# Stick-breaking attention on one core: the order of VectorE, ScalarE and GpSimd written out, v turned inside the score banks, weight units prepared in three steps, 51 tiles for activations

## Chip, core and metric

The kernel runs on one NeuronCore of a Trainium2 chip. The metric is the device time of one execution in microseconds (us). All arithmetic is float32: where TensorE takes part, a value is split into a high part (rounded to the matmul's fp32r format) and a low part (what the rounding left), and a product is three matmuls: low weight times high activation, high times low, high times high.

## The reference, cut to what matters

A decoder trunk of two layers over 512 tokens of width 1024: a Mamba-2 layer, then a stick-breaking attention layer with 16 heads of 64. Each layer ends with a convolutional GLU feed-forward (2816 wide) and a gated per-layer embedding. K and V come from the normed output of layer 0. The part that the change touches:

```python
def stick_breaking_attention(q, k, v):
    scale = SB_HEAD_DIM ** -0.5
    for blk in range(seq // SB_BLOCK):
        ...
        z = jnp.einsum("bthd,bshd->bhts", q[:, q0:q1], k[:, :q1]).astype(jnp.float32) * scale
        causal = (q0 + jnp.arange(SB_BLOCK))[:, None] > jnp.arange(q1)[None, :]
        log_beta = jax.nn.log_sigmoid(z)
        log_keep = jnp.where(causal, jax.nn.log_sigmoid(-z), 0.0)
        log_rest = lax.cumsum(log_keep, axis=3, reverse=True) - log_keep
        w = jnp.where(causal, jnp.exp(log_beta + log_rest), 0.0)
        outs.append(jnp.einsum("bhts,bshd->bthd", w.astype(v.dtype), v[:, :q1]))
```

## The kernel before

Activations lie transposed, features on the 128 partitions and the 512 tokens along the free axis, so that one activation tile is 128x512 float32. All weights stream once from HBM as 240 units of eight 128x128 blocks (512 KB each) in the order in which TensorE uses them (`PLAN`). `Weights.make` loads a unit into `raw` (three buffers, queue of SyncE), multiplies in the gain of a norm where the unit belongs to q, k or v (L95, GpSimd, one instruction for a whole unit), copies it to `whi` (L106, ScalarE) and writes the rest to `wlo` (L107, VectorE). `product` adds up one 128x512 output tile in a bank of PSUM, three matmuls for each 128 rows (L217 to L219), so a unit is 24 matmuls.

In attention a pair is two heads, and there are eight pairs. PSUM has eight banks: two rotating `acc` banks for projections, four `aux` banks and the two banks of `two`. For one pair the kernel makes the scores in five tiles `z` (`scores`: tile 0 takes columns 0 to 255 of both banks of `two`, tiles 1 to 4 an `aux` bank each); ScalarE takes Abs and Exp of each tile (L805, L806), then Ln (L809); VectorE forms softplus (L812) and rounds it (`sh`, L816), and GpSimd writes the rest (`sl`, L817); TensorE adds the cumulative sums into the same banks (`att_b`, L844); ScalarE takes Exp (L847) and rounds (`wh`, L849), VectorE writes the rest (`wl`, L850). The output matmuls of a pair (`att_c`, one call for each head, L868) are issued in the stretch of the next pair, and are evacuated by a ScalarE copy (L873) and a VectorE add (L874).

TensorE's order is written out by hand, for the whole kernel. In the stretch of a middle pair p it is: scores(p), att_c of pair p-1 for head 0, the projection k(p+1), att_c for head 1, the projection q(p+1) with the four transposes of v (L748) after its fourth step, att_b(p), the projection v(p+1). Each of `pav`, k, `pav`, q, `pv` (the transposed v) and v takes the next `acc` bank, in turns of two. k and q are evacuated by one VectorE instruction (L736) that multiplies with the norm's `n_kv.r`, then split by L198 (ScalarE) and L199 (VectorE). The order on VectorE, ScalarE and GpSimd is found by the framework's list scheduler, from the program's order, priorities (`high_priority`) and estimated times. Ahead of the pairs, layer 0's gate phase (`layer_tail`, L687 to L706: one projection a tile, then L694, L695, L698, L701, and the norm's running sum L236 on GpSimd) hands over to q(0), k(0) and k(1); between them come the norm's `sums` (L243) and `spread` (L278), whose result scales q and k.

Of the kernel before, what the change touches and what calls it, by code (L numbers as in the profile page):

```python
# [15 lines left out]
P = 128  # L16
T = 512
NCH = 4
# [49 lines left out]
class Weights:  # L68
# [3 lines left out]
    def __init__(self, tc, pool, src, ahead=2):  # L72
        self.tc, nc = tc, tc.nc
        self.nc, self.pool, self.src, self.ahead = nc, pool, src, ahead
        self.units, self.made, self.pos, self.gains = {}, 0, 0, {}

    def make(self, u, between=None):
        nc = self.nc
# [21 lines left out]
        name = PLAN[8 * u][0]  # L100
        hi = self.pool.tile([P, 8, P], F32R, tag="whi", name="whi", bufs=3)
        lo = self.pool.tile([P, 8, P], F32R, tag="wlo", name="wlo", bufs=3)
        for c, part in enumerate(parts):
            e = nc.gpsimd if u == 0 and c else nc.vector
            with self.tc.high_priority(offset=120) if name == "in" and u > 2 else nullcontext():
                nc.scalar.copy(out=hi[:, part], in_=raw[:, part])  # L106
                e.tensor_tensor(out=lo[:, part], in0=raw[:, part], in1=hi[:, part].bitcast(F32), op=ALU.subtract)  # L107
        self.units[u] = (hi, lo)

    def next(self, what):  # L110
        assert PLAN[self.pos] == what, (PLAN[self.pos], what)
        u, i = divmod(self.pos, 8)
        while self.made < min(NUNIT, u + 1 + self.ahead):
            self.make(self.made)
            self.made += 1
# [6 lines left out]
def tile_yoco(ctx: ExitStack, tc: tile.TileContext, xT, pT, prm, cst, csb, wdt, wts, out, dbg=None):  # L122
# [24 lines left out]
    def H(dt=F32, shape=(P, T), name="h"):  # L147
        return sb.tile(list(shape), dt, tag="H", name=name, bufs=44)
# [31 lines left out]
    wt.made = 1  # L180
# [546 lines left out]
    qs, ks, vs = {}, {}, {}  # L727
# [6 lines left out]
    def qk_split(dst, p, acc, scale):  # L734
        t = S("t", 2)
        V.scalar_tensor_tensor(out=t, in0=acc, scalar=scale, in1=n_kv.r, op0=ALU.mult, op1=ALU.mult)  # L736
        dst[p] = split(t)

    def v_evac(p, acc):
        t = S("t", 2, name="v")  # L740
        V.tensor_tensor(out=t, in0=acc, in1=n_kv.r, op=ALU.mult)
        vs[p] = t

    def v_split(p):
        t = vs[p]
        pv = acc_bank("pv")
        for c in range(NCH):
            PE.transpose(out=pv[:, c * P:(c + 1) * P], in_=t[:, c * P:(c + 1) * P], identity=ident)  # L748
        pv4 = pv.rearrange("p (c i d) -> p c i d", c=NCH, i=2)
        vs[p] = []  # L750
        for i in range(2):
            vv = H(F32R, shape=(P, NCH, 2, 64), name="vv")
            A.copy(out=vv[:, :, 0], in_=pv4[:, :, i])
            V.tensor_tensor(out=vv[:, :, 1], in0=pv4[:, :, i], in1=vv[:, :, 0].bitcast(F32), op=ALU.subtract)
# [6 lines left out]
    def scores(p):  # L761

        two = two_banks("z")
# [35 lines left out]
    def att_a(p):  # L799

        es, sp = {}, {}
        zs = scores(p)
        for n in (2, 0, 1, 3, 4):
            e = es[n] = S("d", 6, name="e") if n < 3 else S("c", 3, name="e")
            A.activation(out=like(n, e), in_=zs[n], func=AF.Abs)  # L805
            last = A.activation(out=e, in_=e, func=AF.Exp, scale=-1.0)  # L806
        with tc.issue_after(last.ins):
            for n in (2, 0, 1, 3, 4):
                ln = A.activation(out=es[n], in_=es[n], func=AF.Ln, bias=1.0)  # L809
        for n in (2, 0, 1, 3, 4):  # L810
            e = es[n]
            V.scalar_tensor_tensor(  # L812
                out=like(n, e), in0=zs[n], scalar=0.0, in1=like(n, e), op0=ALU.max, op1=ALU.add
            )
            hi, lo = H(F32R, name="sh"), H(F32R, name="sl")
            V.tensor_copy(out=hi, in_=e)  # L816
            G.tensor_tensor(out=lo, in0=e, in1=hi.bitcast(F32), op=ALU.subtract)  # L817
            sp[n] = (hi, lo)
        return zs, sp, ln

    def att_b(p, zs, sp, ln):
# [10 lines left out]
        for n in (1, 0, 2, 3, 4):  # L832
# [12 lines left out]
            w = S("c", 3, name="w")  # L845
            with tc.issue_after(ln.ins):
                A.activation(out=like(n, w), in_=z, func=AF.Exp)  # L847
            hi, lo = H(F32R, name="wh"), H(F32R, name="wl")
            A.copy(out=hi, in_=w)  # L849
            V.tensor_tensor(out=lo, in0=w, in1=hi.bitcast(F32), op=ALU.subtract)  # L850
            ws[n] = (hi, lo)
# [6 lines left out]
    def att_c(p, i, ws, bank=acc_bank):  # L858

        if i == 0:  # L860
            ots[p] = S("e", 3)
        ot = ots[p]
# [4 lines left out]
        for n, (o_, l_, r_) in enumerate(mm):  # L867
            PE.matmul(  # L868
                o_, lhsT=l_.rearrange("p a d -> p (a d)"), rhs=r_, start=n == 0, stop=n == len(mm) - 1,
            )  # L870
        tp = S("th", 1, name="tp")
        with tc.high_priority(offset=300):
            A.copy(out=tp[0:64], in_=po[64:128])  # L873
            V.tensor_tensor(out=ot[LO[i]], in0=po[0:64], in1=tp[0:64], op=ALU.add)  # L874
        if i:
            if dbg:
                dbg("o", p, ot)
            o_t.append(split(ot, lo=S("ot", 8, F32R)))

    def qk(name, dst, p, scale, hooks=None):  # L880
        acc = proj(name, p, hooks)
        with tc.high_priority(offset=200):
            qk_split(dst, p, acc, scale)

    def v_proj(p):
        acc = proj("v", p)
        with tc.high_priority(offset=200):
            v_evac(p, acc)
# [6 lines left out]
    qk("k", ks, 1, 1.0, hooks={3: n_kv.spread})  # L895
    with tc.high_priority(offset=400):
        qk_split(qs, 0, qa, 0.125)
        qk_split(ks, 0, ka, 1.0)
    ws = None
    for p in range(8):  # L900
        zz = att_a(p)
# [120 lines left out]
```

## Time and profile before

| what | us |
|---|---|
| three timed executions | 1584.12, 1590.03, 8543.81 (median 1590.03) |
| the profiled execution's own time | 1585.07 |
| its span, first to last instruction | 1583.1 |
| TensorE busy in it | 1508.4 (95%) |
| VectorE, ScalarE, GpSimd busy | 1020.1, 754.4, 344.3 |
| the eight pairs of attention, 842.45 to 1108.00 | 265.55 |

The profile is of one execution. A matmul's end is modelled, so two matmuls in a row overlap in it, and what one costs is read from the distance of their starts. The profile's clock column is TensorE's granted clock as a share of 2.4 GHz: 0.50 is 1.2 GHz.

### The profile page before, as it was taken

To read this page: it belongs to the slowest core of one execution; us is meant where nothing else is said; L and a number is where in the kernel's file an instruction comes from. 1 tells how busy PE (TensorE), PEld (TensorE's weight loads), DVE (VectorE), ACT (ScalarE), POOL (GpSimd) and SP (SyncE) were. 2 spreads that over 40 slices of the span, in tenths; PEclk is the share of its full clock that TensorE was granted. 3 is DMA by queue.
4 is the path that set the end of the run, shared out by engine and by line. 5 is a ranking of instruction groups with operands and counts; after the bars stand their busy time and mean duration, and the time that the engine had idled before them with its cause. 6 is when DMAs were issued, how large, how long until landed. Compare 5 with 4: busy or idle time off the path is not lost.

```text
span 1583.1 us, 18438 instructions
## 1 busy us (share of the span) xinstructions
PE 1508.4 (95%) x7082; PEld 1237.3 (78%) x7082; DVE 1020.1 (64%) x1334; ACT 754.4 (48%) x1152; POOL 344.3 (22%) x243
## 2 busy tenths in 40 slices
PE   7999889999999999999988998897999999999996
PEld 5878668788888888888877777776788888888885
DVE  7987888763677666523585766765566776652444
ACT  4466566533444444323444777666444443342343
POOL 3022342432110110011163433421211101010112
PEclk9999999999999999999998999899999999999998
DMA  5334333333333333333321111111233333333331
GB/s 176 94 125 134 101 100 113 100 98 102 93 94 94 98 102 93 109 103 95 94 81 54 53 54 40 41 57 38 76 94 100 97 93 101 99 100 95 98 87 53
DMA packets 44055, 143.67 MB, mean 91 GB/s; under 512 B 4896, under 2 KB 5152, under 8 KB 43968
## 3 DMA queue, kind: packets, MB, share of 16 engines
q1 hardware_dynamic: 43968, 142.51, 29.1%
q8 instruction: 55, 0.90, 0.2%
q14 instruction: 32, 0.26, 0.1%
HBM read 140.32 MB, written 2.16 MB: 90 GB/s over the span
## 4 chain that ended last, share of the span: by engine, by line
PE 72%; DVE 11%; ACT 8%; issue 4%; POOL 4%; DMA 1%; SPq 0%; POOLq 0%; ACTq 0%; DVEq 0%
PE acc L217 22%; PE acc L219 22%; PE acc L218 22%; PE z L844 3%; DVE wlo L107 2%; DVE c L331 2%; ACT d L499 1%; POOL y L527 1%; ACT whi L106 1%; DVE sh L816 1%; DVE e L812 1%; ACT e L805 1%; PE z L790 1%; ACT e L806 1%; DVE t L698 1%
## 5 line engine op out<-in xcount | busy, mean ns | idle before, releaser
L217 PE MATMUL acc<-hi,wlo 128*128 128x512 f32 x1776 | 710.5, 400 | 26.7 <-DVE t L736 19.9
L218 PE MATMUL acc<-lo,whi 128*128 128x512 f32 x1808 | 708.6, 392 | 0.0
L219 PE MATMUL acc<-hi,whi 128*128 128x512 f32 x1776 | 698.5, 393 | 0.0
L107 DVE TENSOR_TENSOR wlo<-raw,whi 128x1024 fp32r<-128x1024 f32 (+1 forms) x240 | 307.6, 1282 | 199.3 <-ACT whi L106 196.7
L217 PEld LDWEIGHTS acc<-hi,wlo 128*128 128x128 f32 x1776 | 337.7, 190 | 100.0 <-DVE t L736 20.7
L106 ACT CAST whi<-raw 128x1024 fp32r<-128x1024 f32 (+1 forms) x241 | 252.1, 1046 | 330.6 <-PE acc L219 274.9
L218 PEld LDWEIGHTS acc<-lo,whi 128*128 128x128 f32 x1808 | 342.8, 190 | 72.0 <-issue 2.9
L219 PEld LDWEIGHTS acc<-hi,whi 128*128 128x128 f32 x1776 | 337.5, 190 | 72.3
L331 DVE SCALAR_TENSOR_TENSOR c<-t,pm,c 128x511 f32<-128x511 f32 (+2 forms) x248 | 186.7, 756 | 4.8 <-ACT c L326 0.9
L236 POOL TENSOR_TENSOR acc_sq<-acc_sq,sq 128x512 f32<-128x512 f32 x60 | 87.6, 1461 | 403.2 <-ACT sq L233 351.2
L649 POOL TENSOR_TENSOR hf<-th,c 128x512 f32<-128x512 f32 x44 | 59.2, 1346 | 427.7 <-DVE c L331 388.2
L326 ACT ACTIVATE c<-t,pm 128x512 f32<-128x512 f32 x112 | 91.1, 815 | 23.9 <-DVE t L324 23.8
L324 DVE TENSOR_TENSOR t<-acc,r 128x512 f32<-128x512 f32 x112 | 76.7, 686 | 29.5 <-PE acc L219 26.0
L817 POOL TENSOR_TENSOR sl<-e,sh 128x512 fp32r<-128x512 f32 x40 | 57.2, 1432 | 86.2 <-DVE sh L816 83.1
L198 ACT CAST hi<-hf 128x512 fp32r<-128x512 f32 x44 | 26.8, 618 | 95.0 <-POOL hf L649 95.0
L95 POOL TENSOR_TENSOR raw<-raw,pm 128x1024 f32<-128x1024 f32 (+3 forms) x27 | 53.0, 1967 | 84.0 <-DMA raw<-in_wts 77.6
L199 DVE TENSOR_TENSOR lo<-hf,hi 128x512 fp32r<-128x512 f32 x44 | 32.3, 738 | 59.2 <-ACT hi L198 59.2
L646 ACT ACTIVATE th<-c 128x512 f32<-128x512 f32 x44 | 27.8, 632 | 80.8 <-DVE c L331 80.8
L647 DVE SCALAR_TENSOR_TENSOR th<-th,c 128x512 f32<-128x512 f32 x44 | 30.4, 692 | 30.6 <-ACT th L646 30.6
L233 ACT ACTIVATE sq<-x_k 128x512 f32<-128x512 f32 (+1 forms) x50 | 30.5, 615 | 34.5 <-DVE x_k L285 20.8
L850 DVE TENSOR_TENSOR wl<-w,wh 128x512 fp32r<-128x512 f32 x40 | 33.6, 852 | 19.3 <-ACT wh L849 19.3
L499 ACT ACTIVATE d<-d,tok 128x128 f32<-128x128 f32 x128 | 43.5, 390 | 4.1 <-DMA d<-rows 3.4
(193 smaller groups left out, 1507.3 us busy)
## 6 DMA issues: line engine op xcount, KB each, us to landing
raw<-in_wts SPq DMA_DIRECT2D x239, 512.0 KB, 3.6
d<-rows SPq DMA_DIRECT2D x32, 256.0 KB, 3.9
x_k<-in_xT SPq DMA_DIRECT2D x16, 256.0 KB, 4.7
out<-xo SPq DMA_DIRECT2D x8, 256.0 KB, 2.9
p_k<-in_pT SPq DMA_DIRECT2D x4, 256.0 KB, 3.4
raw<-in_wts SPq DMA_DIRECT2D x2, 256.0 KB, 4.0
pm<-in_prm SPq DMA_DIRECT2D x1, 312.0 KB, 6.5
cbt<-in_csb SPq DMA_DIRECT2D x1, 256.0 KB, 4.0
```

Of the source, the lines that this page charges most:

```text
L106: nc.scalar.copy(out=hi[:, part], in_=raw[:, part])
L107: e.tensor_tensor(out=lo[:, part], in0=raw[:, part], in1=hi[:, part].bitcast(F32), op=ALU.subtract)
L217: PE.matmul(acc, lhsT=wl, rhs=xh, start=start and n == 0, stop=False)
L218: PE.matmul(acc, lhsT=wh, rhs=xl, start=False, stop=False)
L219: PE.matmul(acc, lhsT=wh, rhs=xh, start=False, stop=stop and n == len(ks) - 1)
L236: G.tensor_tensor(out=self.acc, in0=self.acc, in1=t, op=ALU.add)
L324: V.tensor_tensor(out=t, in0=acc, in1=r, op=ALU.mult)
L326: A.activation(out=c, in_=t, func=AF.Identity, scale=w[:, f * taps + taps - 1:f * taps + taps], bias=b[:, f:f + 1])
L331: V.scalar_tensor_tensor(out=c[:, s:], in0=t[:, :T - s], scalar=w[:, i:i + 1], in1=c[:, s:], op0=ALU.mult, op1=ALU.add)
L499: A.activation(out=d[:, cs], in_=d[:, cs], func=AF.Relu, scale=-1.0, bias=acs[:, c * 32 + h:c * 32 + h + 1])
L649: G.tensor_tensor(out=hf, in0=th, in1=c1, op=ALU.mult)
L817: G.tensor_tensor(out=lo, in0=e, in1=hi.bitcast(F32), op=ALU.subtract)
```

## The change

- **Order.** A new function `pair` writes out one pair for all engines, and a manual schedule is set on TensorE, VectorE, ScalarE and GpSimd around the eight pairs: each engine then issues its instructions as the program lists them. The list puts the evacuation of k after softplus tile 2 and its rounding, ahead of the other four tiles. Splits are cut into `high` (ScalarE) and `low` (VectorE), which stand in different places. `att_c` is parted from its evacuation `o_evac`. Outside the pairs the list scheduler still decides.
- **v.** The four transposes go to columns 256 to 511 of the two banks of `two` (`v_turn`, no `acc` bank), and are read from there (`v_split`). An accumulation bank is then taken by `pav`, k, `pav`, q and v alone.
- **Weight units.** `make` is cut into `load` (the transfer and the gain), `high` and `low`. Within the pairs `next` makes nothing any more; `pair` loads the next three units (one in the last pair) at its start and places their `high` and `low` steps.
- **Gains.** For the first four units of q, k and v (the two that q(0) and k(0) share, k(1) and v(0)) the gain is multiplied in by ScalarE, eight instructions of 128x128 a unit, in place of GpSimd.
- **First pair.** q(0) and k(0) are evacuated and split in a hook of the projection k(1), right after `spread`.
- **Space.** The common pool of activation tiles has 51 buffers, it had 44; a scratch of the DMA descriptors is cut to 1024 bytes.

```diff
+        self.act_until = PLAN.index(("k", 0, 1)) // 8 + 2
...
     def make(self, u, between=None):
+        self.load(u, between)
+        self.high(u)
+        self.low(u)
...
-            nc.gpsimd.tensor_tensor(
-                out=raw[:, i:i + n], in0=raw[:, i:i + n],
-                in1=self.gains[name][:, k:k + n].unsqueeze(2).to_broadcast([P, n, P]), op=ALU.mult
-            )
+            if u < self.act_until:
+                for j in range(i, i + n):
+                    nc.scalar.activation(
+                        out=raw[:, j], in_=raw[:, j], func=AF.Identity, scale=self.gains[name][:, k + j - i:k + j - i + 1]
+                    )
+            else:
+                nc.gpsimd.tensor_tensor(
...
-        return sb.tile(list(shape), dt, tag="H", name=name, bufs=44)
+        return sb.tile(list(shape), dt, tag="H", name=name, bufs=51)
...
+    def v_turn(p):
+
+        pv = twos[p][:, :, 256:512]
+        for c in range(NCH):
+            PE.matmul(
+                pv[:, c // 2, c % 2 * P:(c % 2 + 1) * P], lhsT=vs[p][:, c * P:(c + 1) * P], rhs=ident,
+                is_transpose=True, start=False, stop=False, skip_group_check=True,
+            )
...
-        pv = acc_bank("pv")
-        for c in range(NCH):
-            PE.transpose(out=pv[:, c * P:(c + 1) * P], in_=t[:, c * P:(c + 1) * P], identity=ident)
-        pv4 = pv.rearrange("p (c i d) -> p c i d", c=NCH, i=2)
+        pv4 = twos.pop(p)[:, :, 256:512].rearrange("p a (c i d) -> p a c i d", c=2, i=2)
...
+    TILES = (2, 0, 1, 3, 4)
+
+    def pair(p, ws, accs):
+
+        zs = scores(p)
+        new = [wt.made + i for i in range(3 if p < 7 else 1)]
+        for u in new:
+            wt.load(u)
...
+        exps(2)
+        exps(0)
+        if p:
+            po = att_c(p - 1, 0, ws)
+        exps(1)
+        if p:
+            o_evac(p - 1, 0, po)
+        exps(3)
+        exps(4)
+        if p == 0:
+            acc = proj("v", 0)
+        elif p < 7:
+            acc = proj("k", p + 1)
+        if p:
+            po = att_c(p - 1, 1, ws)
+        for n in TILES:
+            A.activation(out=es[n], in_=es[n], func=AF.Ln, bias=1.0)
+        sums(2)
+        parts(2)
+        if p == 0:
+            v_evac(0, acc)
+        elif p < 7:
+            kt = qk_evac(acc, 1.0)
+        sums(0)
+        sums(1)
+        parts(0)
+        if 0 < p < 7:
+            kt = high(kt)
+        if p:
+            o_evac(p - 1, 1, po)
+        sums(3)
+        parts(1)
+        sums(4)
+        wt.high(new[0])
+        if p:
+            oh = high(ots[p - 1])
+        if p < 7:
+            acc = proj("q", p + 1, hooks={4: partial(v_turn, p)})
+        else:
+            v_turn(p)
+            for m in range(2):
+                accs.append(acc_bank())
+                product(accs[m], "o", m, range(6), o_t, stop=False)
+        v_split(p)
+        parts(3)
+        parts(4)
+        if p < 7:
+            wt.high(new[1])
+            qt = high(qk_evac(acc, 0.125))
+        ws = att_b(zs, sp)
+        wt.low(new[0])
+        ws[1] = low(*ws[1])
+        if 0 < p < 7:
+            ks[p + 1] = low(*kt)
+        ws[0] = low(*ws[0])
+        if p < 7:
+            qs[p + 1] = low(*qt)
+        ws[2] = low(*ws[2])
+        if p:
+            o_t.append(low(*oh, lo=S("ot", 8, F32R)))
+        ws[3] = low(*ws[3])
+        if p < 7:
+            wt.low(new[1])
+            wt.high(new[2])
+        ws[4] = low(*ws[4])
+        if p < 7:
+            wt.low(new[2])
+            v_evac(p + 1, proj("v", p + 1))
+        return ws
...
+    def first():
+        n_kv.spread()
+        with tc.high_priority(offset=400):
+            qs[0] = split(qk_evac(qa, 0.125))
+            ks[0] = split(qk_evac(ka, 1.0))
+
+    acc = proj("k", 1, hooks={3: first})
...
+    wt.ahead = -1
+    with tc.manual_schedule(engines={mybir.EngineType[e] for e in ("PE", "DVE", "Activation", "Pool")}):
+        for p in range(8):
+            ws = pair(p, ws, accs)
+    wt.ahead = 2
...
-    nc = _bacc.Bacc("TRN2", target_bir_lowering=False, num_devices=1)
+    nc = _bacc.Bacc("TRN2", target_bir_lowering=False, num_devices=1, dynamic_dma_scratch_size=1024)
```

In `pair`, `exps(n)` is Abs and Exp of tile n on ScalarE, `sums(n)` is softplus on VectorE (before: L812), and `parts(n)` is the rounding on VectorE and the rest on GpSimd (before: L816, L817).

## Rows read from the trace of the kernel before

**Rows 1.** The page: the chain that ended last, shares of the span.

```profile
PE 72%; DVE 11%; ACT 8%; issue 4%; POOL 4%; DMA 1%; SPq 0%; POOLq 0%; ACTq 0%; DVEq 0%
```

**Rows 2.** TensorE's waits, 817.16 to 1136: total us, times, longest us.

```profile
PE acc L217 <- DVE t L736: 19.9, 6, 3.3
PE acc L217 <- DVE vv L754: 5.3, 1, 5.3
PE z L778 <- DVE t L736: 4.7, 2, 3.7
PE nsum L243 <- POOL acc_sq L236: 3.8, 1, 3.8
```

**Rows 3.** Stretches: length, busy us by engine (instructions), PEclk, DMA share, GB/s.

```profile
817.16:842.45 25.29, 21.26 (x83) 16.93 (x82) 16.20 (x20) 6.86 (x10) 12.26 (x7) 0.87 0.26 83
842.45:876.18 33.73, 28.44 (x143) 23.13 (x142) 23.16 (x28) 21.79 (x36) 14.95 (x9) 0.90 0.16 48
876.18:1075.14 198.96, 179.09 (x949) 151.39 (x948) 136.46 (x170) 137.14 (x223) 69.19 (x44) 0.93 0.15 48
1075.14:1108.00 32.86, 24.72 (x130) 20.40 (x129) 16.84 (x22) 20.41 (x34) 6.82 (x5) 0.90 0.10 32
```

**Rows 4.** The same view inside pair 5, cut at TensorE's wait, att_b and v.

```profile
1009.87:1020.92 11.05, 11.05 (x71) 9.30 (x69) 3.87 (x6) 10.13 (x17) 1.90 (x1) 1.00 0.17 48
1020.92:1024.24 3.32, 0.00 (x2) 0.00 (x1) 3.32 (x7) 2.22 (x5) 2.35 (x2) 0.92 0.00 0
1024.24:1026.96 2.72, 2.72 (x6) 2.15 (x7) 2.69 (x4) 0.59 (x1) 1.87 (x3) 0.50 0.02 6
1026.96:1031.61 4.65, 4.65 (x23) 3.85 (x22) 4.62 (x6) 0.99 (x2) 2.74 (x2) 0.98 0.28 59
1031.61:1036.85 5.24, 5.24 (x37) 4.90 (x36) 3.30 (x6) 4.71 (x7) 0.00 (x0) 1.00 0.35 124
1036.85:1042.38 5.53, 5.53 (x27) 4.57 (x27) 3.23 (x5) 4.21 (x8) 0.00 (x0) 1.00 0.06 24
```

**Rows 5.** Timeline of ScalarE in pair 5: start, us, instruction [idle before, releaser].

```profile
1011.76 0.60 ACT L805 ACTIVATE e<-z 128x512 f32<-128x512 f32 x1 [0.64 <-PE z L790]
...
1018.98 2.71 ACT L809 ACTIVATE e<-e 128x512 f32<-128x512 f32 x5
```

**Rows 6.** Timeline of VectorE in pair 5.

```profile
1019.65 1.29 DVE L812 SCALAR_TENSOR_TENSOR e<-z,e 128x512 f32<-128x512 f32 x2 [2.31 <-ACT e L809]
1020.85 0.42 DVE L816 CAST sh<-e 128x512 fp32r<-128x512 f32 x1
...
1021.79 1.20 DVE L816 CAST sh<-e 128x512 fp32r<-128x512 f32 x1
...
1023.51 0.67 DVE L736 SCALAR_TENSOR_TENSOR t<-acc,r 128x512 f32<-128x512 f32 x1
```

**Rows 7.** Timeline of GpSimd in pair 5.

```profile
1016.16 1.90 POOL L95 TENSOR_TENSOR raw<-raw,pm 128x1024 f32<-128x1024 f32 x1 [7.91 <-DMA raw<-in_wts]
1021.44 1.27 POOL L817 TENSOR_TENSOR sl<-e,sh 128x512 fp32r<-128x512 f32 x1 [3.38 <-DVE sh L816]
```

**Rows 8.** Timeline of VectorE in the gate phase, GpSimd free.

```profile
792.43 0.69 DVE L698 SCALAR_TENSOR_TENSOR t<-t,pp 128x512 f32<-128x512 f32 x1
...
796.73 1.23 DVE L107 TENSOR_TENSOR wlo<-raw,whi 128x1024 fp32r<-128x1024 f32 x1 [0.44 <-ACT whi L106]
```

**Rows 9.** The chain of waits at the gate phase's end: start, us, what.

```profile
822.69 1.55 DVE wlo L107
824.24 2.32 DVE t L698
```

**Rows 10.** Timeline of GpSimd and ScalarE in the same stretch.

```profile
823.11 2.88 POOL L95 TENSOR_TENSOR raw<-raw,pm 128x1024 f32<-128x1024 f32 x1
...
827.30 0.62 ACT L198 CAST hi<-x_k 128x512 fp32r<-128x512 f32 x1 [4.12 <-DVE x_k L701]
```

**Rows 11.** Timeline of ScalarE in layer 0: a run of 128x128 activations.

```profile
125.87 1.26 ACT L499 ACTIVATE d<-d,tok 128x128 f32<-128x128 f32 x4
```

**Rows 12.** The page: issues of transfers, count, KB each, us to landing.

```profile
raw<-in_wts SPq DMA_DIRECT2D x239, 512.0 KB, 3.6
```

More of the change, by code (lines that the diff above doesn't have):

```diff
@@ L74, in __init__, with load @@
         self.nc, self.pool, self.src, self.ahead = nc, pool, src, ahead
-        self.units, self.made, self.pos, self.gains = {}, 0, 0, {}
+        self.units, self.raws, self.made, self.pos, self.gains = {}, {}, 0, 0, {}
+        self.act_until = PLAN.index(("k", 0, 1)) // 8 + 2
     def make(self, u, between=None):
+        self.load(u, between)
+        self.high(u)
+        self.low(u)
+    def load(self, u, between=None):
         nc = self.nc
@@ L752, in v_split @@
             vv = H(F32R, shape=(P, NCH, 2, 64), name="vv")
[L753 to L754 removed]
+            v5 = vv.rearrange("p (a c) h d -> p a c h d", a=2)
+            A.copy(out=v5[:, :, :, 0], in_=pv4[:, :, :, i])
+            V.tensor_tensor(
+                out=v5[:, :, :, 1], in0=pv4[:, :, :, i], in1=v5[:, :, :, 0].bitcast(F32), op=ALU.subtract
+            )
             vs[p].append(vv)
@@ L797, in like, with att_b @@
         return t.rearrange("p (a b) -> p a b", a=2) if n == 0 else t
[L799 to L821, printed above, removed]
+    def att_b(zs, sp):
         s2, sa, sc = sp[0], sp[1], sp[2]
@@ L844, in att_b @@
                 PE.matmul(o_, lhsT=l_, rhs=r_, start=False, stop=k == len(mm) - 1, skip_group_check=True)
[L845 to L851, printed above, removed]
+            w = S("d", 6, name="w") if n < 3 else S("c", 3, name="w")
+            A.activation(out=like(n, w), in_=z, func=AF.Exp)
+            ws[n] = high(w)
         return ws
@@ L870, in att_c, with o_evac @@
             )
+        return po
+    def o_evac(p, i, po):
+        if i == 0:
+            ots[p] = S("e", 3)
         tp = S("th", 1, name="tp")
[L872 to L888, printed above, removed]
+        A.copy(out=tp[0:64], in_=po[64:128])
+        V.tensor_tensor(out=ots[p][LO[i]], in0=po[0:64], in1=tp[0:64], op=ALU.add)
+        if dbg and i:
+            dbg("o", p, ots[p])
+    TILES = (2, 0, 1, 3, 4)
[4 more added lines that the diff above has]
+            wt.load(u)
+        es, sp = {}, {}
+        def exps(n):
+            es[n] = S("d", 6, name="e") if n < 3 else S("c", 3, name="e")
+            A.activation(out=like(n, es[n]), in_=zs[n], func=AF.Abs)
+            A.activation(out=es[n], in_=es[n], func=AF.Exp, scale=-1.0)
+        def sums(n):
+            V.scalar_tensor_tensor(
+                out=like(n, es[n]), in0=zs[n], scalar=0.0, in1=like(n, es[n]), op0=ALU.max, op1=ALU.add
+            )
+        def parts(n):
+            sp[n] = H(F32R, name="sh"), H(F32R, name="sl")
+            V.tensor_copy(out=sp[n][0], in_=es[n])
+            G.tensor_tensor(out=sp[n][1], in0=es[n], in1=sp[n][0].bitcast(F32), op=ALU.subtract)
+        exps(2)
[67 more added lines that the diff above has]
+        return ws
@@ L894, in tile_yoco @@
     product(ka, "k", 0, [7], xg, start=False)
[L895 to L901, printed above, removed]
[L902 to L920 removed]
+    def first():
[4 more added lines that the diff above has]
+    acc = proj("k", 1, hooks={3: first})
+    with tc.high_priority(offset=200):
+        ks[1] = split(qk_evac(acc, 1.0))
+    ws, accs = None, []
+    wt.ahead = -1
[3 more added lines that the diff above has]
+    wt.ahead = 2
     for m in range(2):
@@ L927, in tile_yoco @@
         if m == 4:
-            att_c(7, 0, ws, aux_bank)
-            att_c(7, 1, ws, aux_bank)
+            for i in range(2):
+                po = att_c(7, i, ws, aux_bank)
+                with tc.high_priority(offset=300):
+                    o_evac(7, i, po)
+            o_t.append(split(ots[7], lo=S("ot", 8, F32R)))
     nrm = Norm(1024, 1e-6, KD)
```

72 lines of the change are left out of this document (34 added, 38 removed).

## Prediction

> **What bounds the kernel now.** I read the chain of waits first: TensorE carries 72% of it [rows 1], so the question is where TensorE stands still or runs at half clock. The view of its waits answers the first half: from 817.16 to 1136 us it waits 20 us, in six equal waits of 3.3, for VectorE's L736, and 14 us more in three other places [rows 2]. The stretches [rows 3] then give the size of attention: six middle pairs take 198.96 us, 33.2 each, pair 0 takes 33.73, pair 7 32.86, and the hand-over ahead of them 25.29. One middle pair cut at its wait [rows 4] shows both halves: 11.05 us of scores, att_c and k at full clock, 3.32 us of nothing, 2.72 us in which the granted clock is 0.50 (1.2 GHz), and then 4.65, 5.24 and 5.53 us at or very near full clock. What it would take without the wait is 11.05 + 2.72/2 + 4.65 + 5.24 + 5.53 = 27.83 us. No other engine is near that: VectorE is busy 136.46/6 = 22.7 us a pair, ScalarE 137.14/6 = 22.9, GpSimd 11.5 [rows 3].
>
> Why the wait: q needs the acc bank that k filled. k is done at about 1019.5, but its evacuation stands sixth on VectorE, at 1023.51 + 0.67 [rows 6], behind softplus and rounding that the list scheduler put first, one of them 1.20 us long where it is 0.42 with GpSimd idle [rows 6, 7].
>
> **The change, part by part.** The sum is made against the profiled execution, 1585.07 us (span 1583.1 and 2.0 around it). It lies near the lowest of the three runs (1584.12); the median, 1590.03, is 5 above it, and a run of 8544 is no measure of the kernel.
>
> *Middle pairs.* TensorE's work is unchanged: the same matmuls in the same order, and four transposes in either case. What changes is when the bank comes free. Softplus of tile 2 can't start earlier than now, since ScalarE's list ahead of it is the same ten passes, one copy, the table load and the first Ln: 1019.65 - 1009.87 = +9.78 into the pair. Behind it now stand one rounding and then k: 9.78 + 0.65 + 0.42 + 0.67 = +11.52, against TensorE's arrival at q at +11.05 [rows 4, 6]. So 0.47 us of the 3.32 stays. I expect no half clock after so short a stop.
>
> What is late next? I walk the lists on from +11.5 with a softplus at 0.6 (1.29 for two), a rounding at 0.4 and a rest on GpSimd at 1.27 [rows 6, 7], and let a rounding wait for a rest that runs. VectorE: softplus 0 and 1 to 12.7, rounding 0 to 13.1, the add of `pav` and softplus 3 to 14.3, rounding 1 to 14.7, softplus 4 to 15.3, v's two halves to 16.1, rounding 3 to 16.5, rounding 4, behind the rest of 3, to 18.2, q to 18.8. GpSimd's rests of tiles 1 and 4 so end at 16.0 and 19.5. TensorE ends q at 11.5 + 0.3 + 5.5 = 17.3 and begins att_b; it comes to tile 4 four us later, covered by 1.8 us. ScalarE rounds q to 19.4, loads its table (7.22 us from the first Abs to the first Ln less eleven passes of 0.54 leave 1.3 [rows 5]) and takes ten passes of 0.54 for Exp and rounding: 26.1, so the banks are free before scores(p+1) at +28; the third unit's copy ends at 27.2. Last comes VectorE: five rests of w, k, q and o at 0.7 and three units at 1.23 [rows 8] follow ScalarE, the third unit ends at +28.5 at the earliest; with one GpSimd gain of 1.90 in its way, and a second, it reaches the end of v_evac between +29.1 and +32.4, that is 1 to 4.2 us into the next pair, and k(p+2) wants v's bank 4.2 us into it. That cover is thin; I charge 0.4 for it (bounds 0 and 0.8). A pair becomes 27.83 + 0.47 + 0.40 = 28.7, and six of them 172.2: **26.8 us saved**.
>
> The weight units' steps, moved: the three transfers are issued from SyncE's queue at the pair's start, where nothing else is queued; the three gains of 1.90 us [rows 7] stand in GpSimd's list ahead of the first rest `sl`. The third waits for raw, freed by the last-but-one VectorE instruction of the pair before, at up to +3.5; 0.3 for the issue, 3.6 to land [rows 12] and 1.90 make +9.3, against the first `sl` at +10.8. Covered by 1.5 us; without cover it is the first rival.
>
> *v in the score banks.* It takes the bank of `pv` out of the turn of two. In exchange the transposes write a tile that ScalarE's Abs and VectorE's softplus of tile 0 read, and stand behind them if the banks are kept apart as one tile. In a middle pair softplus 0 ends at +12.2 and the transposes come at 11.5 + 4 steps of 5.53/8 = +14.3: nothing. In the first and last pair it shows, below.
>
> The trace of before has no row for such a wait. The Trainium skill, "PSUM — Partial Sum Buffer", section "PSUM bank collisions raise a hardware error", says that PSUM is to be guarded by bank and quadrant, and not by address, as two engines in one bank collide even in different columns. That speaks against spare columns as free space. By it the waits below stand; without it the third rival holds.
>
> *Hand-over (25.29).* TensorE loses the 3.8 us wait for the norm's sum [rows 2] and half of the time at the low clock: at a mean of 0.87 [rows 3] some 26% of 21.26 us, 5.5, ran at half, 2.8 lost. Together 6.6. The sum is late because VectorE falls behind in the gate phase: beside a GpSimd gain of 2.88 us its L107 and L698 take 1.55 + 2.32 [rows 9, 10], and 1.23 + 0.69 alone [rows 8]. Four units freed of that give 4 x 1.95 = 7.8 us, more than the delay. ScalarE pays 8 x 1.26/4 = 2.5 us a unit [rows 11]; it stands idle 4.12 us a tile before L198 [rows 10]. If the list scheduler puts the gains into that idle time, they are free; if it puts them between VectorE's steps, a tile gets 2.5 - 1.95 = 0.55 longer and the sum up to 2.2 later than now. The idle row is the nearer one: **6.0 saved**, bounds 6.6 and -2.2.
>
> *Pair 0 (33.73).* Now scores wait 4.7 us for q(0) and k(0) [rows 2], and at a clock of 0.90 [rows 3] 20% of 28.44 us ran at half: 2.8 lost. Evacuated during k(1), some 4 us earlier, both are ready at the pair's start; k(1) itself isn't needed before pair 1. New waits: the transposes behind softplus 0 (+11.5 against +11.1, 0.4) and att_b behind the rest of tile 1 (0.6). 7.5 - 1.0 = **6.5 saved**, bounds 4 and 7.5.
>
> *Pair 7 (32.86).* It has no k and no q to hide anything. Scores and both att_c take 11.05 - 5.53 = 5.5; then TensorE stands until softplus 0, at 9.78 + 0.65 + 0.42 + 0.6 = +11.4. Transposes 0.4, the first 36 matmuls of o at 5.53/24, 8.3, half clock again as in a middle pair 1.4, att_b 5.24: 26.8. **6.0 saved**, bounds 4 and 12. It removes the 5.3 us wait for `pv` [rows 2] and puts one of nearly 6 us earlier.
>
> *The rest.* Outside the pairs the work is the same; 51 tiles and shifted priorities can make the list scheduler order other stages anew. I take 0, bounds of one wait of the size of the sum's, 3.8, either way. The scratch: 0, all weight transfers are issued by SyncE, not by GpSimd.
>
> **Sum.** 6.0 + 6.5 + 26.8 + 6.0 = 45.3; 1585.07 - 45.3 = 1539.8, say 1540 us.
>
> **Rivals.**
> 1. *The ring closes.* Fixed lists block: the last `low` of a unit late on VectorE, so the transfer, so GpSimd's third gain, so the first `sl`, so VectorE's later rows and the bank of v. For it speaks how thin the covers are (1.5 us on GpSimd, at most 3 us for v's bank) and that a rounding beside GpSimd is three times as long [rows 6]; against it, that no engine passes 23 us of busy time in 28.7 [rows 3]. If a wait of 2.0 us and 1.36 of half clock [rows 4] come back in pairs 0 to 6 in place of the 0.87 charged: 7 x 2.5 = 17 us, 1557.
> 2. *Gains on ScalarE fall into the gate phase's path*: the hand-over gives nothing, 1546.
> 3. *The transposes aren't held by tile 0*: pair 7 stands only until att_b's operands come, 5.5 + 0.4 + 8.3, then att_b, some 20 us. Another 6.5 saved: 1533.
> 4. *The order doesn't do what it says*: k's evacuation still waits, for instance for its buffer `t`, and half of the middle pairs' gain is lost: 1553.
> 5. *Slower.* The ring of the first rival not only closes but sets the pair. Added up from my walk it is 24.5 us long (transfer and gain 5.8, five rests 8.7, then att_b's last tile, Exp, rounding and the weights' last split 10), under the 28.7 of TensorE. It decides from 28.7 on, and beats the kernel before only from 35 us a pair; at 37.5, with VectorE's roundings and splits and GpSimd's rests all stretched as the 1.20 us row is, seven pairs cost 62 us more than forecast: 1602.
>
> **How the numbers follow.** Forecast 0.45, rival 1 0.20, rival 2 0.15, rival 3 0.09, rival 4 0.07, rival 5 0.04. The forecast's own bounds are 1532 to 1550. The range takes in rivals 2 and 3 and most of rivals 1 and 4: 1531 to 1562, leaving out rival 5 and the ends of the first. A measurement of this kernel can tell some 2% from no change, which lies at 1558 from the median and at 1553 from the profiled time; half of rivals 1 and 4 lies beyond. Faster by over 2%: 0.45 + 0.15 + 0.09 + about 0.11 = 0.80; slower 0.04; the rest, 0.16, the same.
>
> **What the profile after would show.** Starts of pairs 28 to 29 us apart; the wait for k's evacuation at 0.3 to 0.6 us, six times; no stretch at 0.50 inside the middle pairs; one wait of about 6 us in pair 7 for softplus 0; no wait for the norm's sum, and for q(0) and k(0) none above 0.5; VectorE's last evacuation of a pair after the next pair's start. The prediction is wrong if a wait of 1 us or more comes back in each pair (for GpSimd's rests, or for v's bank), if clocks stay at 0.93 over the middle pairs without such a wait, or if stages outside 817 to 1108 move by more than 4 us.

## The result, and the profile after

The changed kernel takes 1544.47 us (median of 4 runs, 1542.6 to 1545.98) where the kernel before, on the same chip, takes 1588.72: a ratio of 0.9738, 95% interval 0.9726 to 0.9749. One run of the kernel before, of 8543.81 us, lifts that median and is left out of the ratio. 1540 was forecast, in a range of 1531 to 1562. The profiled execution has a span of 1540.6 us, against 1583.1 before.

The view of stretches, cut at the same events as [rows 3] (the first q product, the first matmul of the scores of pairs 0, 1 and 7, the first matmul into `acc_o`, at 1107.96 before) and with a last line for all that follows. After the length come busy times of TensorE, its weight loads, VectorE, ScalarE and GpSimd with their instructions, then the granted clock, DMA share and GB/s:

```profile
816.78:834.78 18.00, 18.00 (x84) 14.63 (x83) 14.03 (x20) 7.06 (x10) 9.53 (x6) 1.00 0.30 84
834.78:862.04 27.26, 25.86 (x144) 21.17 (x143) 17.87 (x24) 21.50 (x34) 11.57 (x7) 1.00 0.07 24
862.04:1037.16 175.12, 167.35 (x949) 142.61 (x948) 114.26 (x171) 139.80 (x222) 73.38 (x45) 1.00 0.18 55
1037.16:1067.08 29.92, 22.83 (x130) 19.42 (x129) 14.34 (x24) 21.31 (x34) 7.29 (x5) 0.89 0.22 70
1067.08:1540.60 473.52, 457.28 (x2029) 377.75 (x2027) 268.78 (x347) 186.95 (x244) 64.57 (x48) 0.99 0.30 91
```

Read it against [rows 3]: the hand-over gives 25.29 - 18.00 = 7.3 us, pair 0 6.5, the six middle pairs 198.96 - 175.12 = 23.8, pair 7 2.9. All ahead of the first q product is 817.16 - 816.78 = 0.4 shorter, and what follows pair 7 is 473.5 us long where it was 1583.10 - 1108.00 = 475.1. The sum is 42.5, the difference of the spans. The last 1.6 are no gain of the change: behind the same wait of 2.5 us this execution goes on at full clock, and others don't, whatever their lists in the pairs (last section); the median lies 1.9 us above this execution. In the first four stretches VectorE needs 160.5 us where it needed 192.7: most of its work is the same and is less often stretched.

TensorE's waits, over the whole span (total us, times, longest us); against [rows 2] L761 is k's evacuation, and L782 are v's transposes:

```profile
PE acc L242 <- DVE t L761: 7.8, 6, 1.3
PE z L782 <- DVE e L911: 7.6, 2, 6.7
...
PE z L864 <- POOL sl L918: 0.6, 2, 0.4
PE nsum L268 <- POOL acc_sq L261: 0.4, 1, 0.4
```

The six waits are still there, 1.3 us each and not 3.3, and the clock of the middle pairs is 1.00 where it was 0.93. In pair 5, timeline of TensorE (start, us, instruction [idle before, releaser]):

```profile
991.16 0.50 PE L242 MATMUL acc<-hi,wlo 128*128 128x512 f32 x1 [1.30 <-DVE t L761]
991.50 0.39 PE L243 MATMUL acc<-lo,whi 128*128 128x512 f32 x1
...
994.02 0.60 PE L782 MATMUL z<-ct,v 128*128 128x128 f32 x4
```

No matmul behind the wait is longer than at full clock. Why 1.30 and not 0.47 is in the lists of ScalarE and VectorE of the same pair, which starts at 978.81:

```profile
980.70 0.60 ACT L907 ACTIVATE e<-z 128x512 f32<-128x512 f32 x1 [2.99 <-PE z L832]
981.33 0.63 ACT L908 ACTIVATE e<-e 128x512 f32<-128x512 f32 x1
981.87 0.58 ACT L907 ACTIVATE e<-z 128x512 f32<-128x512 f32 x1
982.48 0.63 ACT L908 ACTIVATE e<-e 128x512 f32<-128x512 f32 x1
...
986.68 0.64 ACT L908 ACTIVATE e<-e 128x512 f32<-128x512 f32 x1
```

```profile
989.36 0.69 DVE L911 SCALAR_TENSOR_TENSOR e<-z,e 128x512 f32<-128x512 f32 x1 [3.77 <-ACT e L936]
990.08 0.43 DVE L917 CAST sh<-e 128x512 fp32r<-128x512 f32 x1
990.43 0.68 DVE L761 SCALAR_TENSOR_TENSOR t<-acc,r 128x512 f32<-128x512 f32 x1
```

An Exp begins 0.6 us behind the Abs that it reads, the next Abs 0.54 behind that Exp. So softplus 2 starts at 989.36 - 978.81 = +10.55, not at the +9.78 of [rows 6]; rounding and k follow as forecast.

In the hand-over, VectorE's gate phase (compare the stretched rows of [rows 9]) and ScalarE beside it:

```profile
808.67 0.68 DVE L723 SCALAR_TENSOR_TENSOR t<-t,pp 128x512 f32<-128x512 f32 x1
...
812.69 1.25 DVE L134 TENSOR_TENSOR wlo<-raw,whi 128x1024 fp32r<-128x1024 f32 x1 [0.45 <-ACT whi L126]
```

```profile
807.93 2.43 ACT L104 ACTIVATE raw<-raw,pm 128x128 f32<-128x128 f32 x8
810.26 0.60 ACT L223 CAST hi<-x_k 128x512 fp32r<-128x512 f32 x1
```

VectorE's two steps are back near the 0.69 and 1.23 of [rows 8] in the tiles whose gains ScalarE takes; beside the next unit's gain, which stays on GpSimd (817.96), the low half at 818.12 takes 2.81 us. The eight gains of a unit, 2.43 us, stand in what was ScalarE's idle time ahead of the rounding of the tile [rows 10], and end at 810.36, 0.3 us after that tile is ready (809.38 + 0.69).

### The profile page after: what moved, and what is told of

The parts are those of the page before. It is cut to its first block, busy times and chain, and to the rows that moved or that the text cites. A ratio compares the mean times of both kernels' runs of the same rounds, so it can differ in the third digit from the quotient of the medians.

```text
span 1540.6 us, 18399 instructions
## 1 busy us (share of the span) xinstructions
PE 1486.8 (97%) x7082; PEld 1221.1 (79%) x7082; DVE 982.3 (64%) x1334; ACT 769.5 (50%) x1184; POOL 330.5 (21%) x236
## 4 chain that ended last, share of the span: by engine, by line
PE 76%; ACT 9%; DVE 6%; issue 3%; POOL 3%; DMA 0%; POOLq 0%; SPq 0%; ACTq 0%; DVEq 0%
PE acc L242 23%; PE acc L243 23%; PE acc L244 23%; PE z L864 2%; ACT e L908 2%; DVE c L356 1%; ACT e L907 1%; DVE wlo L134 1%; ACT d L524 1%; POOL y L552 1%; ACT e L936 1%; ACT whi L126 1%; ACT L936 1%; POOL d L528 1%; PE z L832 1%
## 5 line engine op out<-in xcount | busy, mean ns | idle before, releaser
L134 DVE TENSOR_TENSOR wlo<-raw,whi 128x1024 fp32r<-128x1024 f32 (+1 forms) x240 | 302.3, 1260 | 190.3 <-ACT whi L126 186.8
L242 PEld LDWEIGHTS acc<-hi,wlo 128*128 128x128 f32 x1776 | 334.3, 188 | 80.1 <-DVE t L761 8.6
L244 PEld LDWEIGHTS acc<-hi,whi 128*128 128x128 f32 x1776 | 333.9, 188 | 70.6
L108 POOL TENSOR_TENSOR raw<-raw,pm 128x1024 f32<-128x1024 f32 x20 | 38.8, 1940 | 60.0 <-DMA raw<-in_wts 44.5
L911 DVE SCALAR_TENSOR_TENSOR e<-z,e 128x512 f32<-128x512 f32 x40 | 26.8, 686 | 32.8 <-ACT e L936 32.5
L258 ACT ACTIVATE sq<-x_k 128x512 f32<-128x512 f32 (+1 forms) x50 | 30.6, 615 | 26.8 <-DVE x_k L310 12.9
```

The lines of the kernel that those rows point to most:

```text
L242: PE.matmul(acc, lhsT=wl, rhs=xh, start=start and n == 0, stop=False)
L244: PE.matmul(acc, lhsT=wh, rhs=xh, start=False, stop=stop and n == len(ks) - 1)
```

## Experiments

The kernel before ran beside each of the experiments, with medians of 1586.0 to 1586.6 us; a change from the changed kernel is taken from stretches of the two traces where it is small, and otherwise the medians stand beside 1544.47. None leaves out a part of the reference.

**k's evacuation later, and earlier.** Two places on VectorE, with ScalarE and GpSimd untouched.

```diff
 # k sixth (pairs 1 to 6)
-        elif p < 7:
-            kt = qk_evac(acc, 1.0)      # behind parts(2)
 ...
-            kt = high(kt)
+            kt = high(qk_evac(acc, 1.0))   # behind sums(0), sums(1), parts(0)
 # k first (pairs 1 to 6)
+        if 0 < p < 7:
+            kt = qk_evac(acc, 1.0)      # ahead of sums(2)
         sums(2)
         parts(2)
 ...
-        elif p < 7:
-            kt = qk_evac(acc, 1.0)
```

> The changed kernel, with k's evacuation put back to the sixth place of VectorE's list in pairs 1 to 6 (behind three softplus steps and three rounding steps, as the list of the kernel before had it). Theory (the gain of a middle pair is the wait of q's product on k's bank, with the half clock that follows it): the wait goes from 1.30 us to some 4 us in each of the six pairs, and a stretch at half clock follows it again; 16 to 24 us slower, 1560 to 1568 us. Rival (the gain of a pair is the removal of the transposes of v as a stretch of their own with their evacuation and of steps of weights between, and k's place only moves a wait): under 6 us slower.

> The changed kernel, with k's evacuation ahead of the softplus of tile 2 in pairs 1 to 6. Theory (what is left of the wait of q's product is softplus 2 standing ahead of k's evacuation): the wait goes from 1.30 us to near 0.2, softplus 2 and all that follows on VectorE ends some 0.6 us later, and nothing waits for that: 5.5 to 7 us faster, some 1538 us. Rival (the ring of the score banks closes: rounding 2 is later, so the parts of the scores' second half and TensorE's next step wait): within 2 us of the changed kernel, with the wait on another line.

With k sixth the median is 1564.14 us (1560.75 to 1566.2), 19.7 longer; with k first 1536.21 (1535.35 to 1539.9), 8.3 shorter. With k sixth, one pair of TensorE's timeline:

```profile
1006.26 0.50 PE L242 MATMUL acc<-hi,wlo 128*128 128x512 f32 x1 [3.00 <-DVE t L761]
...
1007.75 0.61 PE L242 MATMUL acc<-hi,wlo 128*128 128x512 f32 x1
1008.16 0.63 PE L243 MATMUL acc<-lo,whi 128*128 128x512 f32 x1
```

The wait is 3.00, less than the 4 expected. The edit puts k behind three softplus steps and two roundings; the expectation counted three roundings, and in the kernel before it stood behind four softplus steps and two roundings, with the 3.3 us. Behind the wait matmuls of 0.39 become 0.63 until the transposes: from the end of the wait to the next pair's start that is 1024.66 - 1006.26 = 18.40 us, in the changed kernel 1007.98 - 991.16 = 16.82. So 1.7 us of wait cost 1.6 us of clock as well, and this pair is 32.45 us long instead of 29.18. With k first, a whole pair as one stretch:

```profile
976.20:1004.15 27.95, 27.95 (x159) 23.73 (x158) 19.63 (x29) 23.20 (x37) 13.39 (x8) 1.00 0.21 57
```

TensorE is busy for all of it. The softplus and rounding steps that are later cost little: att_b takes 5.51 us (993.11 to 998.62) where the changed kernel takes 5.25 (968.04 to 973.29), and the starts move apart at the last tile's rest. In the six pairs that is 7.4 us, and the theory of k's place holds in both directions, inside these lists.

**k's place alone, in the kernel before.** Only softplus and rounding are issued behind k's evacuation.

```diff
-        zz = att_a(p)
+        zs, es, ln = att_a(p)              # without softplus and rounding
 ...
+            kev = qk("k", ks, p + 1, 1.0)
+            with tc.issue_after(kev.ins):
+                sp = att_a2(zs, es)        # softplus and rounding
```

> The kernel before, with one thing altered: in pairs 1 to 6 the softplus and rounding steps are issued behind k's evacuation, so that VectorE's list has it ahead of the first softplus. Nothing else of the change is in it. Theory (the gain of the middle pairs is k's place): the wait of q's product, 3.3 us a pair, goes under 0.5, and so does the stretch at half clock behind it; 18 to 24 us faster than the kernel before, 1562 to 1569 us. Rival (without a fixed list for ScalarE and GpSimd, and with v's own bank, the softplus steps are now late and the scores' parts wait instead): less than 10 us faster, with waits on the lines of the scores' parts or of v's transposes.

1579.49 us (1577.86 to 1579.69) against 1586.03: ratio 0.9957, interval 0.9941 to 0.9973. The theory fell here, and the rival's waits are in the trace (TensorE's, whole span; then the first middle pair and all six as stretches):

```profile
PE z L850 <- POOL sl L823: 9.5, 11, 0.9
PE pv L749 <- DVE e L880: 7.7, 7, 1.9
...
PE z L850 <- DVE sh L822: 3.2, 6, 0.6
```

```profile
875.99:907.92 31.93, 28.69 (x159) 23.54 (x158) 23.49 (x28) 21.49 (x37) 14.48 (x9) 1.00 0.17 50
...
875.99:1068.48 192.49, 174.75 (x949) 144.07 (x948) 137.42 (x170) 132.95 (x223) 74.96 (x44) 0.98 0.16 50
```

The 3.3 us wait is gone from all six pairs. In four of them it comes back as pieces of 1.0 (the transposes wait for a bank that VectorE's add of `pav` frees; the add now stands behind k's rest, for which VectorE waits 1.6 us on ScalarE's rounding), 0.5, 0.9 and 0.8 (att_b waits for rounding and rest), 3.2 in a pair, at full clock. In the other two the first three pieces are the same, then the clock falls inside att_b and the pair takes 32.4 us; in the third middle pair:

```profile
961.35:965.00 3.65, 3.65 (x15) 3.26 (x15) 3.65 (x5) 1.63 (x4) 3.22 (x2) 0.54 0.54 145
```

What is gained, 198.96 - 192.49 = 6.5 us, is less than what the half clock behind the one long wait had cost, six times 1.36 [rows 4].

**The lists of the three engines back to the list scheduler, all else as changed.**

```diff
-    with tc.manual_schedule(engines={mybir.EngineType[e] for e in ("PE", "DVE", "Activation", "Pool")}):
+    with tc.manual_schedule(engines={mybir.EngineType[e] for e in ("PE",)}):
```

> The changed kernel, with only TensorE's list fixed in the pairs: those of VectorE, ScalarE and GpSimd are the list scheduler's again. Theory (the gain of the middle pairs comes from the fixed place of k's evacuation): 15 to 30 us slower, 1560 to 1575 us, with the wait of q's product over 2 us in most pairs. Rival (the split of the weight units and the bank of v carry it, and the scheduler now finds a list as good): within 5 us.

1571.85 us (1567.86 to 1575.88). Hand-over, pair 0 and the six middle pairs:

```profile
819.06:837.08 18.02, 18.02 (x84) 14.62 (x83) 14.05 (x20) 7.06 (x10) 9.61 (x6) 1.00 0.30 86
837.08:864.94 27.86, 26.12 (x144) 21.23 (x143) 22.89 (x26) 20.81 (x34) 15.34 (x9) 1.00 0.21 61
864.94:1063.32 198.38, 178.22 (x950) 149.79 (x949) 123.40 (x169) 137.12 (x222) 74.43 (x43) 0.94 0.16 48
```

The middle pairs lose their whole gain (198.38 against 198.96 before), with a wait of 3.4 us in each; the hand-over and pair 0 keep theirs to within 0.6, and pair 7 takes 29.31 us. So the lists carry the middle pairs and nothing else, and v's spare bank and the split units bring nothing there without them.

**The parts that stand beside the lists.** Four kernels, each with one part undone:

```diff
 # weight units whole: each low right behind its high
         wt.high(new[0])
+        wt.low(new[0])
 ...
             wt.high(new[1])
+            wt.low(new[1])
 ...
 # v in a bank of its own
-        pv = twos[p][:, :, 256:512]
+        twos[p] = pv = acc_bank("pv")
 ...
 # gains on GpSimd
-        self.act_until = PLAN.index(("k", 0, 1)) // 8 + 2
+        self.act_until = 0
 # q(0), k(0) late: their evacuations issued behind k(1), no longer inside it
-    acc = proj("k", 1, hooks={3: first})
+    acc = proj("k", 1, hooks={3: n_kv.spread})
 ...
```

> The changed kernel, with the low half of each of the three weight units of a pair made right behind its high half, as the kernel before made them, in the fixed lists. Theory (the split of the units has no part in the gain: VectorE has some 10 us of idle time in a pair, and 1.2 us earlier or later in its list delays nothing that ends last): within 1.5 us of the changed kernel. Rival (the 1.2 us ahead of the last two rounding steps and of q's evacuation make the parts of the scores late): 0.5 to 1.2 us in each pair, 3.5 to 9 us slower, with a wait of the scores' parts on GpSimd in each pair.

1552.22 us (1550.01 to 1553.27), 7.7 longer; pair 0 takes 29.10 us instead of 27.26 and a middle pair 30.03 instead of 29.18. The rival was right, and the idle time of VectorE was the wrong thing to count. TensorE's waits for the rest of a tile go from 0.6 us in two places to

```profile
PE z L864 <- POOL sl L918: 3.4, 8, 0.4
```

because the low halves now fall among GpSimd's rests and take twice the 1.21 us that they take alone (VectorE, one pair):

```profile
970.51 2.00 DVE L134 TENSOR_TENSOR wlo<-raw,whi 128x1024 fp32r<-128x1024 f32 x1
...
974.30 2.32 DVE L134 TENSOR_TENSOR wlo<-raw,whi 128x1024 fp32r<-128x1024 f32 x1
```

The first of them stands ahead of the roundings of tiles 3 and 4, which so start at 973.63, +19.2 us into the pair, where the changed kernel has them at +17.5 (996.27 - 978.81); GpSimd's rest of the last tile is late by as much. All of the 0.85 us of a pair lies in att_b, which takes 5.25 us in the changed kernel and here

```profile
972.82:978.91 6.09, 5.66 (x38) 4.97 (x36) 3.96 (x6) 2.96 (x4) 4.72 (x3) 1.00 0.51 140
```

Half of it shows as the wait of 0.4; by the starts of the matmuls 0.7 of it lie at the last tile's rest. In this pair k's product also starts later, at +4.40 and not +4.17, behind v's evacuation, but q's starts at +12.34 as before, so that costs nothing. Pair 0 has a further wait of 1.3 us, for v's halves.

> The changed kernel, with v transposed into a bank of its own among the accumulator banks again, the rest as in the changed kernel. Theory (the spare half of a score bank only removes one more user of the accumulator banks, and k never waited for it): within 1.5 us in the middle pairs; the 0.85 us and 6.75 us that the transposes wait behind softplus 0 in the first and the last pair go, of which the first is a gain of 0.9 us at most and the second moves to the next products: 1540 to 1545 us. Rival (the bank is what the middle pairs gain from: with it the q product or the transposes wait for a bank again): 2 to 4 us a pair, 1556 to 1568 us.

1548.27 us (1546.34 to 1549.42), 3.8 longer. The six middle pairs take 175.06 us, the same: there the bank is worth nothing once the lists are fixed. The cost is in pair 7, where the 6.75 us wait of the transposes becomes two:

```profile
PE acc L242 <- DVE e L888: 6.7, 1, 6.7
...
PE pv L782 <- DVE e L888: 1.2, 1, 1.2
```

With `pv` in the turn of two, it takes the bank that the first tile of the o product had, and that tile takes the bank of head 1's `pav` and waits for its add (L888). Pair 7 is 1070.40 - 1037.84 = 32.6 us long instead of 29.9. I expected the wait to move, not to grow. The kernel before took 32.86 there, so most of what the change gains in pair 7 is the bank's.

> The changed kernel, with the gains of the first four units of the expert weights back on GpSimd. Theory (the hand-over from the gate to the first pair is shorter because ScalarE takes these gains, so that VectorE's subtractions of the gate don't run beside GpSimd): the stretch of 18.0 us goes back toward 25 us, and the low halves and products of the gate's tiles stretch again from 0.7 to over 2 us; 5 to 8 us slower, 1550 to 1552 us. Rival (the fixed order of the lists outside the pairs made the hand-over shorter): no change, within 1 us.

1551.52 us (1548.65 to 1553.51), 7.0 longer (the four units are those of q, k and v, and not of expert weights). The hand-over is 24.24 us, 6.2 longer, and the norm's sum waits again; pair 0 (27.4) and the middle pairs (29.2) are as in the changed kernel.

```profile
PE nsum L268 <- POOL acc_sq L261: 4.2, 2, 3.8
```

> The changed kernel, with the evacuations of the first q and k products issued behind the second k product again instead of inside it. Theory (pair 0 is shorter because the scores of pair 0 no longer wait for them): a wait of TensorE of 5 to 6 us ahead of the first scores comes back, 5 to 7 us slower, 1549 to 1551 us. Rival (the list scheduler puts them early in either case, and the wait was taken away by the shorter hand-over): within 1 us.

1549.99 us (1548.67 to 1551.07), 5.5 longer. Pair 0 takes 33.12 us, at a clock of 0.90, and its scores wait:

```profile
PE z L820 <- DVE t L761: 4.0, 2, 3.0
```

The hand-over stays at 17.98 (834.56 - 816.58). So the gains on ScalarE make the hand-over and the place of the two evacuations makes pair 0, each by itself.

**44 tiles.**

```diff
-        return sb.tile(list(shape), dt, tag="H", name=name, bufs=51)
+        return sb.tile(list(shape), dt, tag="H", name=name, bufs=44)
```

> The changed kernel, with 44 activation tiles in place of 51. Theory (what is split early in a pair holds up to some 50 tiles, so 44 would make writers of new halves wait for tiles of the pair before): waits in the pairs on tiles that are read late, 5 to 20 us slower. Rival (tiles come free in time even with 44, and the number matters nowhere): within 1.5 us, also outside the pairs.

1545.58 us (1542.96 to 1547.38), 1.1 longer with runs that overlap; pairs of 29.1 to 29.2 us. The seven tiles are worth nothing that can be measured; the theory fell. The smaller scratch of the DMA descriptors was not tried by itself.

**Abs one tile ahead of Exp, and the three together.**

```diff
+        def exp2(n):                       # the Exp, taken out of exps(n)
 ...
         exps(2)
         exps(0)
+        exp2(2)                            # from here each Exp behind the next tile's Abs
 # pair 7, for the three together only
-            v_turn(p)
             for m in range(2):
                 accs.append(acc_bank())
                 product(accs[m], "o", m, range(6), o_t, stop=False)
+                if m == 0:
+                    v_turn(p)
```

> The changed kernel, with ScalarE's absolute value of the next tile put ahead of the exponential of this one, in all pairs. Theory (an exponential that stands right behind the absolute value that it reads starts later on ScalarE, which makes the five pairs of steps some 0.7 us longer, and the logarithm, softplus and k's evacuation with them): the last exponential ends at +7.8 us of a pair and not +8.5, q's product waits 0.5 us and not 1.3; 4 to 5 us faster, some 1540 us. Rival (the row's extra time is the wait for each tile's scores, which the order doesn't change): no change, within 1 us.

> The changed kernel with k's evacuation ahead of softplus 2 in pairs 1 to 6, the absolute values one tile ahead of the exponentials in all pairs, and in the last pair half of the o product ahead of the transposes of v. Theory: the wait of q's product goes (6 x 1.3 us), and the 6.75 us that the transposes wait in the last pair are partly filled by 128 columns' worth of product o; 9 to 12 us faster, 1533 to 1536 us. Rival (once q's product starts earlier the parts of the scores or the weights are late by as much): 1538 to 1541 us, with waits on the scores' parts in the trace.

Abs ahead: 1538.91 us (1538.48 to 1539.36), 5.6 shorter, with a wait of 0.57 us in each of the six pairs and pairs of 28.45:

```profile
PE acc L242 <- DVE t L761: 3.4, 6, 0.6
```

The three together: 1530.37 us (1529.21 to 1530.71), a ratio of 0.9644 to the kernel before (0.963 to 0.9658), the best of all and some 14 us under the changed kernel. ScalarE in pair 5 of the latter:

```profile
974.48 1.09 ACT L907 ACTIVATE e<-z 128x512 f32<-128x512 f32 x2 [2.62 <-PE z L832]
975.45 0.63 ACT L910 ACTIVATE e<-e 128x512 f32<-128x512 f32 x1
975.97 0.60 ACT L907 ACTIVATE e<-z 128x512 f32<-128x512 f32 x1
976.45 0.64 ACT L910 ACTIVATE e<-e 128x512 f32<-128x512 f32 x1
```

and its middle pairs and pair 7 as stretches:

```profile
861.85:1027.94 166.09, 166.09 (x950) 142.38 (x948) 116.89 (x171) 136.50 (x222) 74.05 (x45) 1.00 0.20 58
1027.94:1053.75 25.81, 22.17 (x130) 18.11 (x128) 16.85 (x24) 20.75 (x34) 8.29 (x5) 1.00 0.29 82
```

In the middle pairs TensorE has no idle time left, at full clock: 27.68 us a pair, and only fewer or shorter matmuls would shorten it. Of the 14 us, 9.0 are theirs, 0.7 pair 0's. Pair 7 gave 4.1, more than I expected: its waits are 1.3, 0.3, 1.2 and 0.8 us and not 6.75 and 0.35, and the clock is 1.00 there instead of 0.89.

## Why the prediction was right, point by point

The terms come to 42.5 us in the profiled execution where 45.3 were forecast. The middle pairs and pair 7 gave 3.0 and 3.1 too little; the hand-over and the rest made up 1.3 and 2.0, of which 1.6 were luck.

- **What bounded the kernel** and **a pair without a wait** (27.83 us, worked out from the pieces of one pair): right. Kernels without the wait measure 27.95 and 27.68.
- **Middle pairs**, 26.8 forecast, 23.8 measured: the mechanism held, two sizes did not. The step that softplus of tile 2 "can't start earlier than now", with the same ten passes ahead of it on ScalarE, took the passes' count from [rows 5] and not their order. (In [rows 6] k stands seventh, behind four softplus steps and two roundings, and not sixth; the sum doesn't use it.) The list scheduler had them interleaved; the written list puts each Exp behind its own Abs, and softplus 2 is 0.77 us later. The wait so measures 1.30 where 0.47 was forecast, and putting the Abs ahead gives 0.57. The other way went the charge of 0.40 for v's bank: v was evacuated at 980.98, +2.2, and k came at +4.2 without a wait. 1.30 - 0.87 is 0.43 us a pair, 2.6 of the 3.0 that are missing.
- **No half clock after so short a stop**: right at 1.3 us (clock 1.00); with 3.0 us it is back, in each of six pairs.
- **The transposes guarded as one tile**: right. They waited 0.85 us in pair 0 and 6.75 in pair 7, for softplus 0; forecast were 0.4 and about 6. The third rival is out. The trace agrees with the Trainium skill, "PSUM — Partial Sum Buffer", section "PSUM bank collisions raise a hardware error", by which PSUM is to be guarded by bank and quadrant and not by address. The wait is the program's own; whether the chip needs it no run here shows.
- **Hand-over**, 6.0 forecast, 7.3 measured, above its bound of 6.6: the list scheduler did put the gains into ScalarE's idle time, and the norm's sum came without its wait. The second rival is out: with the gains back on GpSimd 6.2 us are lost. The bound was too low in both its terms: TensorE's idle time there was 25.29 - 21.26 = 4.0 us and not the 3.8 of one wait, and its busy time fell from 21.26 to 18.00, 3.3, where 2.8 were reckoned for the low clock.
- **Pair 0**, 6.5 forecast and measured, shown by its own undoing (5.9).
- **Pair 7**, 6.0 forecast, 2.9 measured, under the bound of 4: the step that failed is the sum of 26.8, which ends with att_b, while the 32.86 us that it was taken from go on to the first `acc_o`, over six more matmuls of o. They take 1067.08 - 1065.03 = 2.05 us, 0.35 of it a wait. The stop, too, ends at +12.3 and not at +11.4, mostly by the same 0.77. 26.8 + 2.05 + 0.9 makes 29.8 of the 29.92. The clock adds chance here: with the same list, pair 7 took 29.85 to 30.85 us in five of the experiments.
- **The rest**, 0 forecast: 2.0 in the profiled execution, of which 1.6 are the clock's chance and not the order's.
- **Rivals 1 and 5**, a ring of transfers, gains and rests that closes: out in the changed kernel, where GpSimd's rests cost TensorE 0.6 us in all. How near it lies was shown: with each weight unit's low half 1.2 us earlier on VectorE a pair is 0.85 us longer, and in the kernel before k's place alone brought the waits back on other lines. What the prediction did not price is that the split of the units is worth about 7 us, by putting those steps behind the last roundings.
- **Rival 4**, k still waits: out; k's place moves the time by 20 and 8 us in the two directions.
- **The signs**: two failed. A wait for k of 1.30 us stayed in each middle pair, where 0.3 to 0.6 was to be seen, and the pairs start 29.2 us apart and not 28 to 29.

## What to carry to other kernels

When an order is written out by hand, walk each engine's list with its dependencies, not with its count of passes: a step that reads the one just ahead of it on the same engine starts later than one with another between. A wait removed by one move in a list comes back on other lines unless the rest of the list is moved with it, so test the move alone and inside the whole. Count, for a step that starts while GpSimd works, its stretched time, even where its engine is idle a third of the pair.

## What the runs showed of the hardware

- A 128x512 pass of ScalarE that reads the result of the pass ahead of it starts 0.61 to 0.63 us behind it; behind a pass that it doesn't read, 0.48 to 0.54. Five such pairs of passes made 0.73 us of TensorE's wait (1.30 against 0.57).
- TensorE's clock stayed at 1.00 behind every wait of 1.3 us in the middle pairs. Behind one wait of 3.0 us (k sixth) matmuls went from 0.39 to 0.63 us in all six pairs, in the one shown some 1.5 us after work resumed, and up to 1.6 us a pair were lost; behind pieces of 0.5 to 1.0 us it happened in two pairs of six (k's place alone), and these lost 1.3. So one wait was dearer than the same time in pieces.
- Chance has a part in it. With the lists back to the scheduler, five of six waits of 3.36 us were followed by the low clock; behind the sixth a pair ran at 1.00 throughout:

```profile
930.90:962.50 31.60, 28.22 (x160) 23.77 (x159) 20.98 (x28) 22.86 (x37) 14.49 (x8) 1.00 0.16 50
```

- The same wait of 2.54 us behind pair 7, at the same place of the same list, was followed by full clock in the changed kernel's execution and by 0.63 us matmuls in that of the three edits together; what follows pair 7 differs by 1.5 us for it (473.5 and 475.0). Over all thirteen profiled executions that stretch is 473.5 us long in five, one of them with k's place alone in the kernel before, and 475.0 to 475.2 in eight. TensorE's timeline, first of the changed kernel and then of the three edits:

```profile
1094.78 0.50 PE L242 MATMUL acc_o<-hi,wlo 128*128 128x512 f32 x1 [2.54 <-DVE x_k L310]
1095.11 0.39 PE L243 MATMUL acc_o<-ot,whi 128*128 128x512 f32 x1
```

```profile
1081.47 0.80 PE L242 MATMUL acc_o<-hi,wlo 128*128 128x512 f32 x1 [2.54 <-DVE x_k L310]
1082.07 0.63 PE L243 MATMUL acc_o<-ot,whi 128*128 128x512 f32 x1
```

- A 128x1024 subtraction on VectorE takes 1.21 to 1.23 us alone, and no longer where a GpSimd instruction starts after it. Where one already runs when it starts, it took from 1.22 to 2.9 us: 2.0 and 2.3 with the units whole, 2.81 in the changed kernel's hand-over, but 1.24 at 998.02 in its pair 5, where two GpSimd rests take 3.56 us and one alone takes 1.30.
